# Order of the work beside the matmuls in the projections of a two-layer encoder step

## The chip, the cores and the metric

The kernel runs on one core of one Trainium2 chip. The metric is the device time of one execution in microseconds (us); less is better. The profile comes from one execution, recorded by the hardware profiler. Its names for the engines: PE is the TensorE's matmul side, PEld its loading of weights, DVE the VectorE, ACT the ScalarE, POOL the GpSimd, SP the SyncE, whose instructions issue DMAs. A suffix q (SPq, POOLq) means an engine's queue. Engines run side by side and wait for each other with semaphores; each works through its own instructions in order.

## The reference

A streaming encoder step of two layers, on a prompt of 2048 frames and 64 new frames of a running stream, with d = 1024, 16 heads of 64. Layer A: RMSNorm, one projection to q, k, v and gate, softmax attention over a band of 9 chunks of 64 frames with a learned bias on the relative distance, gate, output projection, residual. Then one projection to shared keys and values, and layer B: projection to q and gate, strictly causal stick-breaking attention over 2048 cached rows and the new ones, gate, output projection, residual, a last norm.

```python
def a_project(x, g, w_in):
    h = rms_norm(x, g)
    q, k, v, gate = jnp.split(h @ w_in, 4, axis=-1)
    return split_heads(q), split_heads(k), split_heads(v), gate

def shared_kv(x, g, w_kv):
    h = rms_norm(x, g)
    k, v = jnp.split(h @ w_kv, 2, axis=-1)

def sb_block(q, k, v, q_pos, k_pos):
    z = jnp.einsum('bqhd,bkhd->bhqk', q, k).astype(jnp.float32) * SCALE
    mask = (k_pos[None, :] < q_pos[:, None])[None, None]
    log_fail = jnp.where(mask, jax.nn.log_sigmoid(-z), 0.0)
    later = jnp.flip(jnp.cumsum(jnp.flip(log_fail, -1), axis=-1), -1) - log_fail
    w = jnp.where(mask, jnp.exp(jax.nn.log_sigmoid(z) + later), 0.0)
    return jnp.einsum('bhqk,bkhd->bqhd', w.astype(v.dtype), v)
```

The outputs are the two streams after the last norm, and the new keys and values of both layers, for the prompt and for the new frames. All is 32-bit.

## The kernel before

**Stages.** One after the other: the projections of A (about 0 to 760 us of the profiled span), band attention with A's output projection (to about 1497), the projections to the shared keys and values and B's q and gate (to about 2169), stick-breaking attention with the rest (to the end). The change is in the two runs of `projections`.

**Precision.** Every operand of a matmul is kept as two parts, high and low (`h`, `l`), whose sum is the 32-bit value; a `split` is a copy to the high part on ScalarE and a subtraction on VectorE for the low part. A product takes three matmuls for a block of 128 rows of weights: high by high, high by low, low by high.

**The pieces of `projections`.** The prompt is cut into two halves of 1024 frames. For each half:
- *values* (`values`): tiles of 128 frames by 512 columns, 24 matmuls each (`ps_v`). Half 0 has 18 (with the new frames), half 1 has 16. In the meantime the frames are normed (`normed`, GpSimd scales `xt`), transposed (`ps_tr`) and split (`parted`). The weights of values come in blocks (`block_rows`: DMA to `vraw`; `two_blocks`: scaled with the norm's gain to `vwh`, `vwl`). After each value `leave` splits and stores it; in B it stores the raw value (`v_raw<-vn`), and a tick later loads the rows shifted by one (`vps<-v_raw`), subtracts (`less`), splits (`vs`) and stores (`v_b<-vs`), since B's attention works on differences of values that stand next to each other.
- *mixing* (`mix`, beside the values): sums and differences of quarters of the frames, for the next item. Steps `one`, `two`, `three` for each of four pieces.
- *pairs* (`pair`): the columns of two heads for k, q or gate, in the manner of Strassen: P1 to P7, seven products of 12 matmuls instead of eight. Sums `c`, `u2` are made on VectorE. Two of the seven products reuse a PSUM bank, `ps_x` (P1, P3, P5, P7) and `ps_z` (P2, P4), once its content has been copied out (ScalarE, `c<-ps_x`, `c<-ps_z`) or added (VectorE). Half 0 of A has 12 pairs and half 1 has 8, B 12 and 4. In half 0 a pair also holds the 64 new frames (`new_frames`, `ps_q`, after P3). The heads are left as a split (`hl`) and stored by `put`.

**The weights of a pair** go through steps that are named in `weights_of`: `load` (two DMAs to `wraw`), `s1`, `s2` (four scalings each on GpSimd), `b1`, `b2` (splits of the upper and lower half: `ohh`, `ohl`; `olh`, `oll`), `-t1` to `-t4` (differences on GpSimd, written back to `wraw`) and `t1` to `t4` (splits of those; the profile shows `t1` as `x_new` in half 1 and the others as `t`). They are run between the products of earlier pairs: `this` is the pair of the products, `following` the next, `third` the one after; the raw tiles of `third` are those of `this`.

**Staged work.** Between the products, `all_pairs` starts jobs for later stages as room comes: `stage_cache` (loads a block of cached keys to `kr`, a few products later transposes it on TensorE into `ps_c`, splits to `ks`, stores; in A also the values `vr`), `stage_diff` (differences of cached values: `vvp`, `vvr`), `stage_w_out`, `stage_bias` (`bt`, stored to `bias`). A `tick` after each product lets the steps that wait in `waiting` move on.

**What sets the order.** The kernel is scheduled by Tile. A job's first step is its DMA, a later one its arithmetic. Inside `projections`, while `order.on` is set, every instruction on TensorE, VectorE, ScalarE and GpSimd is kept in the order in which the program makes it, and so are the DMAs made with `sp`, which is `order.engine(nc.sync)`. DMAs made with `nc.sync` itself go to the same engine, SyncE, where the scheduler chooses their place among the others. SyncE is one queue: a DMA whose data isn't ready holds what stands behind it.

```python
            def after(n, *steps):

                waiting.append([n, *steps])
                return waiting[-1]

            def tick():
                for x in waiting:
                    x[0] -= 1
                    if x[0] < 0:
                        x.pop(1)()
                        x[0] = 0
```

Of the kernel before, what the change touches and what calls it, by code (L numbers as in the profile page):

```python
# [16 lines left out]
P = 128  # L17
# [107 lines left out]
def encoder_step(ctx: ExitStack, tc: tile.TileContext, a: dict, o: dict):  # L125
# [143 lines left out]
    def projections(L, x_of, begin, w_v, cv, gv, out_v, jobs, first, prompt, sample, stages):  # L269
        with ExitStack() as own, ExitStack() as beside, ExitStack() as early:  # L270
# [61 lines left out]
            def fetched(t, pool, bufs):  # L332
                n = TOK[t][1]
                xt = pool.tile([P, D], F32, name="xt", tag="xt", bufs=bufs)
                sp.dma_start(xt[:n], x_of(t))
                return xt
# [31 lines left out]
            def block_rows(half, j, tag):  # L368
# [3 lines left out]
                sp.dma_start(raw, src.rearrange("(k p) c -> p k c", p=P))  # L372
# [16 lines left out]
            waiting, flight, seqs = [], [], [[*range(NK), len(TOK) - 1], [*range(NK, 2 * NK)]]  # L389
            seq, seq1 = seqs  # L390

            def after(n, *steps):

                waiting.append([n, *steps])
                return waiting[-1]

            def tick():
                for x in waiting:
                    x[0] -= 1
                    if x[0] < 0:  # L400
                        x.pop(1)()
                        x[0] = 0
                waiting[:] = [x for x in waiting if len(x) > 1]

            def values(hf, half, i, t, vws, pool, vps):
# [23 lines left out]
                def leave():  # L429
# [5 lines left out]
                    if L == "a":  # L435
                        store(out, sp.dma_start)
# [7 lines left out]
                    if L == "b":  # L444
                        sp.dma_start(vraw[1 + r0 : 1 + r0 + n, cols], vn)
                    sp.dma_start(dst[:, cols], vn)
                    if L == "a" or half and t in seqs[hf][-2:]:
                        return

                    prev = vps[i % 2]  # L450

                    def load():
                        if t == 0:
                            gps.memset(prev[0:1], 0.0)
                            for x, m in ((0, 112), (112, 15)):
                                sp.dma_start(prev[x + 1 : x + 1 + m], vraw[1 + x : 1 + x + m, cols])
                        elif n == NS:
                            sp.dma_start(prev[0:1], a["cache_b_v"][PAST - 1 : PAST, cols])
                            sp.dma_start(prev[1:n], vraw[1 + r0 : r0 + n, cols])
                        else:  # L460
                            sp.dma_start(prev, vraw[r0 : r0 + P, cols])

                    def less():
                        dve.tensor_tensor(prev[:n], prev[:n], vn, ALU.subtract)
                        store(prev[:n], sp.dma_start)

                    after(1, load, less)
# [3 lines left out]
            def weights_of(kind, w, c0, g, hp, raw, forms):  # L471
# [5 lines left out]
                def load():  # L477
                    for i, r in enumerate(raw):
                        sp.dma_start(r, w[i * CH : i * CH + CH, c : c + 2 * P].rearrange("(k p) c -> p k c", p=P))
# [6 lines left out]
                def whole(i):  # L486
                    split(*forms[i], raw[i].rearrange("p k (b c) -> p b k c", b=2))
                    if (kind, hp) in lay[L]["w"]:
                        for j, part in enumerate(forms[i]):
                            sp.dma_start(f32(lay[L]["w"][kind, hp][j, i]), f32(part))  # L490
# [32 lines left out]
            def pair(hf, kind, c0, hp, forms, pool, this, following, third, event):  # L523
# [14 lines left out]
                def leave(b, t0, src):  # L538
                    at = slice(r0 + t0 * CH, r0 + t0 * CH + CH)
                    hl = pool.tile([P, 2, CH], F32R, name="hl", tag="hl", bufs=HL[L, hf])  # L540
                    if kind == "g":
                        act.activation(f32(hl[:, 0]), src, AF.Silu)
                        sp.dma_start(lay[L]["g"][hp + b][:, at], f32(hl[:, 0]))
# [1527 lines left out]
```

## Time and profile before

| | before |
|---|---|
| median of 3 runs | 3414.68 us |
| lowest, highest run | 3414.37, 3416.91 us |
| the profiled execution | 3414.56 us |
| its span, first to last instruction | 3412.8 us |
| mean granted TensorE clock | 0.974 of full |
| DMA | 684.22 MB, 200 GB/s over the span |

A row of the profile names the line, the engine, the operation, what is written and what is read, and how many. Since nearly every instruction is made in one helper that keeps the order, nearly all rows stand at its line (L114); they are told apart by the names of the tiles. In the view of waits a row `PE ps_x <- ACT c` means that TensorE stood ahead of an instruction on `ps_x` until ScalarE had done one on `c`. In a timeline the number in brackets is the idle time just before the instruction, and after it what ended it.

### The profile page before, as it was taken

To read this page: it belongs to the slowest core of one execution; us is meant where nothing else is said; L and a number is where in the kernel's file an instruction comes from. 1 tells how busy PE (TensorE), PEld (TensorE's weight loads), DVE (VectorE), ACT (ScalarE), POOL (GpSimd) and SP (SyncE) were. 2 spreads that over 40 slices of the span, in tenths; PEclk is the share of its full clock that TensorE was granted. 3 is DMA by queue.
4 is the path that set the end of the run, shared out by engine and by line. 5 is a ranking of instruction groups with operands and counts; after the bars stand their busy time and mean duration, and the time that the engine had idled before them with its cause. 6 is when DMAs were issued, how large, how long until landed. Compare 5 with 4: busy or idle time off the path is not lost. (4 is left out here: it accounts for less than half of the span.)

```text
span 3412.8 us, 52013 instructions
## 1 busy us (share of the span) xinstructions
PE 3178.7 (93%) x16760; PEld 2644.0 (77%) x16760; DVE 2211.5 (65%) x3940; ACT 1870.0 (55%) x3743; POOL 1696.5 (50%) x2381
## 2 busy tenths in 40 slices
PE   7988998799998999997799987999999999999999
PEld 5766786578888888876678776788888887888877
DVE  4555445447777777236454555488887888888883
ACT  3333453337888777223354434366665667666663
POOL 3434535545565545014343325244466777777761
PEclk9989999999999999998899998999999999999999
DMA  4577654669799996446688765877755547455423
GB/s 159 171 254 253 216 182 178 224 213 254 219 255 278 240 234 184 149 158 226 215 304 299 258 237 187 266 218 196 211 171 158 154 110 221 135 159 149 127 76 117
DMA packets 476398, 684.22 MB, mean 200 GB/s; under 512 B 61105, under 2 KB 258257, under 8 KB 476126
## 3 DMA queue, kind: packets, MB, share of 16 engines
q1 hardware_dynamic: 473822, 672.51, 63.9%
q10 hardware_dynamic: 2304, 8.39, 0.7%
q8 instruction: 133, 2.18, 0.3%
q14 instruction: 139, 1.14, 0.1%
HBM read 422.01 MB, written 258.76 MB: 199 GB/s over the span
## 5 line engine op out<-in xcount | busy, mean ns | idle before, releaser
L114 DVE TENSOR_TENSOR pl<-wt,ph 128x512 fp32r<-128x512 f32 (+1 forms) x864 | 551.3, 653 | 108.0 <-ACT ph L114 104.0
L114 ACT ACTIVATE ph<-wt 128x512 fp32r<-128x512 f32 (+1 forms) x864 | 485.1, 578 | 189.8 <-PE wt L114 177.4
L114 PE MATMUL wt<-ident,s 128*128 128x128 f32 x3472 | 551.9, 274 | 9.4 <-DVE pl L114 7.2
L114 PEld LDWEIGHTS wt<-ident,s 128*128 128x128 f32 x3472 | 417.9, 141 | 84.0 <-DVE pl L114 13.1
L114 ACT ACTIVATE f<-z 128x512 f32<-128x512 f32 (+4 forms) x680 | 355.1, 536 | 191.4 <-PE z L114 124.7
L114 POOL TENSOR_TENSOR s<-f,s 128x256 f32<-128x256 f32 x416 | 361.3, 869 | 102.9 <-DVE s L114 94.8
L114 PE MATMUL acc<-ph,vt 128*128 128x512 f32 (+3 forms) x1088 | 374.3, 379 | 6.2 <-ACT ot L114 2.4
L114 PE MATMUL z<-kt,q 128*128 128x512 f32 (+3 forms) x1280 | 372.5, 378 | 3.3 <-ACT f L114 3.0
L114 PE MATMUL acc<-pl,vt 128*128 128x512 f32 (+3 forms) x1088 | 363.3, 367 | 9.3 <-DVE pl L114 9.0
L114 POOL TENSOR_TENSOR two<-f 128x256 f32<-128x256 f32 x416 | 260.1, 627 | 156.0 <-ACT f L114 140.8
L114 DVE TENSOR_TENSOR_SCAN s<-two,s,own 128x256 f32<-128x256 f32 x408 | 299.9, 737 | 34.0 <-POOL two L114 32.6
L114 POOL TENSOR_SCALAR s<-s,rc 128x640 f32<-128x640 f32 (+5 forms) x264 | 201.5, 768 | 235.2 <-DVE rc L114 140.3
L114 POOL TENSOR_TENSOR wraw<-wraw 128x512 f32<-128x512 f32 x96 | 141.3, 1482 | 276.4 <-DVE oll L114 199.4
L114 PEld LDWEIGHTS z<-kt,q 128*128 128x128 f32 x1280 | 220.1, 190 | 33.4 <-ACT f L114 9.9
L114 PE MATMUL ps_x<-x_own,t 128*128 128x512 f32 x864 | 225.6, 411 | 14.1 <-ACT c L114 13.7
L114 DVE CUSTOM_DVE_ANT_0 s<-z,bias 128x640 f32<-128x640 f32 (+4 forms) x256 | 184.7, 733 | 67.8 <-PE wt L114 52.2
L114 PEld LDWEIGHTS acc<-pl,vt 128*128 128x128 f32 x1088 | 193.9, 190 | 42.8 <-DVE pl L114 27.2
L114 DVE TENSOR_TENSOR_SCAN s<-f,own 128x128 f32<-128x128 f32 (+4 forms) x264 | 202.3, 787 | 30.1 <-ACT f L114 29.5
L114 PEld LDWEIGHTS acc<-ph,vt 128*128 128x128 f32 x1088 | 196.6, 190 | 29.0 <-ACT ph L114 8.4
L114 PE MATMUL ps_o<-big,oh 128*128 128x512 f32 x544 | 213.8, 393 | 0.0
L114 PE MATMUL ps_o<-bigl,oh 128*128 128x512 f32 x544 | 213.1, 392 | 0.0
L114 ACT ACTIVATE s<-s,mn 128x640 f32<-128x640 f32 (+5 forms) x264 | 200.4, 761 | 23.0 <-DVE mn L114 22.0
(248 smaller groups left out, 7159.4 us busy)
## 6 DMA issues: line engine op xcount, KB each, us to landing
vt<-v_b SPq DMA_DIRECT2D x80, 512.0 KB, 4.7
v_b<-vs SPq DMA_DIRECT2D x64, 512.0 KB, 3.1
q<-q_a SPq DMA_DIRECT2D x128, 256.0 KB, 5.4
q<-q_b SPq DMA_DIRECT2D x128, 256.0 KB, 4.3
vt<-v_a SPq DMA_DIRECT2D x48, 512.0 KB, 8.0
kt<-k_b SPq DMA_DIRECT2D x96, 256.0 KB, 5.8
v_a<-vs SPq DMA_DIRECT2D x40, 512.0 KB, 4.0
keys<-k_a SPq DMA_DIRECT2D x80, 256.0 KB, 6.9
```

Of the source, the lines that this page charges most:

```text
L114: ins = op(*args, **kwargs)
```

## The change

The edit changes no arithmetic of a matmul: TensorE has as many instructions as before, ScalarE too. VectorE has 2 fewer and GpSimd 2 more (two subtractions of values change engine), SyncE 2 more.

- All DMAs of `projections` and of the staged jobs are made with `nc.sync` instead of `sp`.
- In `pair`, a head's split and store go to a list, `lagging`, and run one product later, behind that product's sum. The weights' differences run about a product ahead of the splits that use them, and `s2` is set apart from `s1`.
- `after` takes a delay for each step. The subtraction on B's values runs two ticks after the load's tick instead of one; the slot of `vps` alternates on across the two column halves.
- The last three values of half 1 in B (before: two) aren't subtracted on the spot but staged (`new_diffs`).
- A mixing step runs with each value instead of two with some; the weight steps of the first pair are spread over more values.
- `bt` gets a second buffer (and `rel` shares it), `nn` loses one. At the start the loads are made where they are used.

```diff
-            def after(n, *steps):
+            def after(*steps):
-                waiting.append([n, *steps])
+                waiting.append([*steps])
                 return waiting[-1]
             def tick():
                 for x in waiting:
                     x[0] -= 1
                     if x[0] < 0:
                         x.pop(1)()
-                        x[0] = 0
+                        x.pop(0)
...
-                        sp.dma_start(vraw[1 + r0 : 1 + r0 + n, cols], vn)
-                    sp.dma_start(dst[:, cols], vn)
-                    if L == "a" or half and t in seqs[hf][-2:]:
+                        nc.sync.dma_start(vraw[1 + r0 : 1 + r0 + n, cols], vn)
+                    nc.sync.dma_start(dst[:, cols], vn)
+                    if L == "a" or half and t in seqs[hf][-3:]:
                         return
-                    prev = vps[i % 2]
+                    prev = vps[(half * len(seqs[hf]) + i) % 2]
...
-                    after(1, load, less)
+                    after(1, load, 1, less)
...
                 def leave(b, t0, src):
...
+                    def two():
+                        at = slice(r0 + t0 * CH, r0 + t0 * CH + CH)
+                        hl = pool.tile([P, 2, CH], F32R, name="hl", tag="hl", bufs=HL[L, hf])
+                        if kind == "g":
+                            act.activation(f32(hl[:, 0]), src, AF.Silu)
+                            nc.sync.dma_start(lay[L]["g"][hp + b][:, at], f32(hl[:, 0]))
+                            return
+                        split(hl[:, 0], hl[:, 1], src)
+                        put(L, kind, hp + b, at, hl)
...
+                    lagging.append(two)
...
                 times(x, quarter(hf, 0, 0), w11, True)
                 c1 = plain(x)
-                run(this, "t3", "t4")
+                run(this, "t2", "-t3")
+                lagged()
                 slot(0)
                 z = psum.tile([P, CH], F32, name="ps_z", tag="mm", bufs=5)
                 times(z, mixed(hf, 0), t1, True)
                 c5 = plain(z)
-                run(third, "load")
+                run(this, "t4")
+                run(following, "s2")
                 slot(1)
                 times(x, mixed(hf, 1), t2, False)
                 u2 = plain(x)
+                run(this, "t3")
                 slot(2)
+                run(third, "load")
                 if hf == 0:
                     nn = new_frames()
-                run(following, "b1", "-t1")
+                run(following, "b1")
                 slot(3)
                 times(z, mixed(hf, 2), w22, False)
                 dve.tensor_tensor(u2, z, u2, ALU.add)
-                rest = leave(1, 0, u2)
-                run(following, "t1")
-                rest()
                 if hf == 0:
                     new_turned(nn)
+                run(following, "-t1")
+                leave(1, 0, u2)
                 slot(4)
                 times(x, mixed(hf, 3), t3, False)
                 dve.tensor_tensor(c5, x, c5, ALU.add)
-                leave(1, 1, c5)()
+                run(following, "t1")
+                lagged()
+                leave(1, 1, c5)
                 slot(5)
                 y = psum.tile([P, CH], F32, name="ps_y", tag="mm", bufs=5)
                 times(y, quarter(hf, 1, 0), w21, True)
                 dve.tensor_tensor(c1, y, c1, ALU.add)
-                rest = leave(0, 0, c1)
-                run(following, "b2", "-t2")
-                rest()
+                run(following, "b2")
+                lagged()
+                leave(0, 0, c1)
+                run(third, "s1")
                 slot(6)
                 times(x, quarter(hf, 1, 1), t4, False)
-                last = plain(x) if kind == "k" and hf * HALF + CH - first >= 0 else x
-                rest = leave(0, 1, last)
-                run(following, "t2", "-t4", "-t3")
-                rest()
-                run(third, "s1", "s2")
+                if kind == "k" and hf * HALF + CH - first >= 0:
+                    x = plain(x)
+                run(following, "-t2", "-t4")
+                lagged()
+                leave(0, 1, x)
                 slot(7)
+                if not following:
+                    lagged()
...
-                    for _ in range((1, 1, 2, 2, 2, 2, 2, 0)[i]):
-                        mixing.pop(0)()
-                    if i == 3:
+                    for _ in range(1 + i % 2):
+                        if mixing:
+                            mixing.pop(0)()
+                    if i == 0:
                         raws = [raw_tiles()]
...
                         run(made[0], "load")
-                    if i == 5:
+                    if i == 2:
                         run(made[0], "s1")
+                    if i == 4:
+                        run(made[0], "b1", "s2")
                     if i == 6:
-                        run(made[0], "b1", "s2", "-t1")
+                        run(made[0], "-t1")
                     if i == 7:
                         run(made[0], "t1")
```

What the scheduler makes of it can be seen in the order of each engine. On SyncE, in A's pairs of half 0, before, where `kr` is the load of cached keys, `ks` their split on its way out, and `hl` a head:

```order
L114 DMA k_a_89<-ks 128x2x512
L114 DMA k_a_89<-hl 128x2x512
L114 DMA kr<-in_cache_a_k 128x4x128
L114 DMA vr<-in_cache_a_v 128x4x128
L114 DMA v_a<-vs 128x4x256
L114 DMA k_a_89<-hl 128x2x512
```

There the first job's `ks` is stored ahead of the second job's load. The same place after the change, where the `kr` is that of the third job:

```order
L911 DMA kr<-in_cache_a_k 128x4x128
L266 DMA k_a_90<-hl 128x2x512
L266 DMA k_a_89<-ks 128x2x512
L266 DMA k_a_90<-hl 128x2x512
L931 DMA v_a<-vs 128x4x256
L914 DMA vr<-in_cache_a_v 128x4x128
```

The load of a block of keys moved up by one job: it stands ahead of the store of the first job's `ks` instead of behind it and a head.

On VectorE, one pair of A's half 1 before, from the sum of P4 (`c<-ps_z`) past those of P5 (`c<-ps_x`) and P6 (`c<-ps_y`):

```order
L114 TENSOR_TENSOR c<-ps_z,c 128x512
L114 TENSOR_TENSOR x_new<-wraw,x_new 128x512
L114 TENSOR_TENSOR hl<-c,hl 128x512
L114 TENSOR_TENSOR vs<-vvp,vs 128x8x64
L114 TENSOR_TENSOR c<-ps_x,c 128x512
L114 TENSOR_TENSOR hl<-c,hl 128x512
L114 TENSOR_TENSOR c<-ps_y,c 128x512
L114 TENSOR_TENSOR oll<-wraw,olh 128x1024
```

And after:

```order
L114 TENSOR_TENSOR c<-ps_z,c 128x512
L114 TENSOR_TENSOR vs<-vvp,vs 128x8x64
L114 TENSOR_TENSOR c<-ps_x,c 128x512
L114 TENSOR_TENSOR x_new<-wraw,x_new 128x512
L114 TENSOR_TENSOR hl<-c,hl 128x512
L114 TENSOR_TENSOR c<-ps_y,c 128x512
L114 TENSOR_TENSOR oll<-wraw,olh 128x1024
L114 TENSOR_TENSOR hl<-c,hl 128x512
```

The cut of `t1` (`x_new`) and the head's rest (`hl`) moved behind the sum of P5.

On GpSimd, in the same pairs before; `x8` scalings are `s1` and `s2`, the others on `wraw` differences, `vvp` staged work:

```order
L114 TENSOR_TENSOR wraw<-wraw 128x4x128 x3
L114 TENSOR_SCALAR wraw<-wraw,g_a 128x256 x8
L114 TENSOR_TENSOR vvp<-vvp,vvr 128x512 x2
L114 TENSOR_TENSOR wraw<-wraw 128x4x128
L114 TENSOR_TENSOR vvp<-vvp,vvr 128x512
```

And after:

```order
L114 TENSOR_SCALAR wraw<-wraw,g_a 128x256 x4
L114 TENSOR_TENSOR vvp<-vvp,vvr 128x512
L114 TENSOR_TENSOR wraw<-wraw 128x4x128 x3
L114 TENSOR_SCALAR wraw<-wraw,g_a 128x256 x4
L114 TENSOR_TENSOR vvp<-vvp,vvr 128x512
L114 TENSOR_TENSOR wraw<-wraw 128x4x128
```

The eight scalings in a row became two lots of four, one ahead of the differences and one behind.

More of the change, by code (lines that the diff above doesn't have):

```diff
@@ L435, in leave @@
                     if L == "a":
-                        store(out, sp.dma_start)
+                        store(out, nc.sync.dma_start)
                     dst = out_v(t)
@@ L489, in whole @@
                         for j, part in enumerate(forms[i]):
-                            sp.dma_start(f32(lay[L]["w"][kind, hp][j, i]), f32(part))
+                            nc.sync.dma_start(f32(lay[L]["w"][kind, hp][j, i]), f32(part))
                 differ = dict(
@@ L552, in rest @@
                             dst = prompt[row : row + CH, (hp + b) * P : (hp + b) * P + P]
-                            after(1, partial(natural, pool, src, 0, P, 4, dst))
-                    return rest
+                            after(0, partial(natural, pool, src, 0, P, 4, dst))
+                    lagging.append(two)
                 def new_frames():
@@ L654, in event @@
                             begin()
-                            flight.append((after(3, *steps), tags))
+                            flight.append((after(3, steps[0], *(x for y in steps[1:] for x in (0, y))), tags))
                     following, third = ([*made[i + 1 :], {}, {}])[:2]
@@ L687, in values_beside @@
                 begin()
-                after(1, *steps)
+                after(1, steps[0], *(x for y in steps[1:] for x in (0, y)))
             todo = [
@@ L738, in projections @@
                         values_beside(i, ("ol", "xr"))
-                    if i in (4, 6):
-                        mixing = mix(0, (i - 4) // 2, [tmp[0], tmp[4 + (i - 4) // 2], tmp[1], tmp[2]])
-                    if 4 <= i < 8:
-                        for x in mixing[:2] if i % 2 == 0 else mixing[2:]:
-                            x()
                     if i == 6:
@@ L751, in projections @@
                     values(0, 1, i, t, vws, pool, vps)()
[L752 to L757 removed]
+                    if mixing:
+                        mixing.pop(0)()
                     if i == 1:
@@ L785, in projections @@
             made += [weights_of(*x, raws[i % 2], forms) for i, x in enumerate(todo[0]) if i]
-            run(made[1], "load", "s1", "s2")
+            run(made[1], "load", "s1")
             spaces = tc.tile_pool(name=f"s0_{L}", bufs=2, side="right")
@@ L887, in projections @@
             staging["pool"] = beside.enter_context(tc.tile_pool(name=f"s1_{L}", bufs=2))
-            run(made[0], "b2", "-t2", "t2", "-t4", "-t3")
-            run(made[1], "load", "s1", "s2")
+            run(made[0], "b2", "-t2", "-t4")
+            run(made[1], "load", "s1")
             all_pairs(1, todo[1], made, forms, spool, staging, {})
+            assert not staged[1]
             while waiting:
@@ L984, in cut @@
             split(vs[:, 0], vs[:, 1], raw)
-            sp.dma_start(f32(wod[k][:, :, cols]), f32(vs))
+            nc.sync.dma_start(f32(wod[k][:, :, cols]), f32(vs))
         return [load, cut]
@@ L1581, in encoder_step @@
     diffs = [("cache", t, i) for t in range(PAST // P) for i in range(2)]
-    new_diffs = [("new", t, 1) for t in (7, 16, 14, 15)]
+    new_diffs = [("new", t, 1) for t in (6, 7, 16, 13, 14, 15)]
     outs = [(k, half) for k in range(NK) for half in range(2)]
@@ L1782, in encoder_step @@
         o["b_k_s"],
[L1783 removed]
+        (beside_b, [staged_b, new_diffs[3:]]),
     )
```

129 lines of the change are left out of this document (58 added, 71 removed).

## The prediction

> **What bounds the kernel now.** I read the shares first, then the stages. The page's line of the TensorE, for the whole span:
>
> ```profile
> PE 3178.7 (93%) x16760; PEld 2644.0 (77%) x16760; DVE 2211.5 (65%) x3940; ACT 1870.0 (55%) x3743; POOL 1696.5 (50%) x2381
> ```
>
> TensorE works 93% of 3412.8 us and the other engines half to two thirds, so what can be gained is TensorE's idle time and its slow matmuls. The change touches the two `projections` stages, so I cut those into pieces with the view of busy time by windows: values of half 0, pairs of half 0, values of half 1, pairs of half 1, for mixer A and then B; the tenth row is one undisturbed pair of A.
>
> ```profile
> 22.30:139.90 117.60, 109.87 (x474) 87.20 (x473) 69.37 (x90) 44.97 (x81) 51.40 (x47) 0.96 0.41 142
> 139.90:455.30 315.40, 281.16 (x1297) 226.29 (x1296) 163.96 (x275) 130.55 (x231) 130.15 (x142) 0.96 0.68 227
> 458.60:564.60 106.00, 95.03 (x433) 76.85 (x431) 51.70 (x83) 42.94 (x76) 45.06 (x47) 0.97 0.51 184
> 564.60:759.80 195.20, 167.56 (x677) 129.84 (x677) 94.24 (x117) 79.45 (x132) 106.67 (x109) 0.96 0.63 215
> 1506.00:1634.90 128.90, 110.65 (x475) 88.67 (x474) 71.85 (x99) 51.09 (x92) 44.53 (x42) 0.89 0.62 213
> 1634.90:1949.10 314.20, 287.10 (x1394) 234.26 (x1393) 156.41 (x211) 145.27 (x250) 128.36 (x141) 0.96 0.78 272
> 1949.10:2071.20 122.10, 98.15 (x434) 78.88 (x432) 63.48 (x95) 45.91 (x81) 44.69 (x44) 0.90 0.65 226
> 2071.20:2168.80 97.60, 90.76 (x401) 72.63 (x401) 48.52 (x57) 44.58 (x74) 41.47 (x43) 0.94 0.60 203
> 413.50:435.20 21.70, 21.70 (x104) 17.74 (x103) 9.25 (x12) 9.95 (x17) 10.17 (x12) 1.00 0.44 153
> ```
>
> The columns are the window's length, busy us of PE, PEld, DVE, ACT and POOL, the granted clock, the DMA share and GB/s. The last row is what a pair of half 0 costs when nothing is waited for: 21.70 us, TensorE busy throughout at clock 1.00. A pair of half 1 has no new frames: seven products. The TensorE's timeline in half 1 of A shows the price of a product, with and without a wait ahead of it:
>
> ```profile
> 635.46 0.50 PE L114 MATMUL ps_x<-big,t 128*128 128x512 f32 x1 [2.89 <-DVE c L114]
> ...
> 639.90 0.40 PE L114 MATMUL ps_x<-big,ohh 128*128 128x512 f32 x1
> ...
> 642.66 2.92 PE L114 MATMUL ps_z<-x_own,x_new 128*128 128x512 f32 x12
> ...
> 652.72 0.73 PE L114 MATMUL ps_z<-x_own,olh 128*128 128x512 f32 x2 [4.35 <-ACT c L114]
> ...
> 657.16 2.96 PE L114 MATMUL ps_x<-x_own,t 128*128 128x512 f32 x12
> ```
>
> P1, from 639.90 to 642.66, takes 2.76 us for twelve matmuls. P7 ahead of it, after a wait of 2.89 us, took 4.44 us (635.46 to 639.90), and so did P4 after 4.35 us (652.72 to 657.16). So a wait of about 3 us or more costs itself **and 1.68 us** of slow matmuls. [...]
>
> With 2.76 us a product a pair of half 1 needs 19.4 us, and with 24 matmuls, 5.5 us, a value. From these, plus the small transposes seen in undisturbed stretches, I estimate what the eight windows would take with no wait: 105.6 (18 values), 267 (12 pairs, 18 cache flips at 0.38), 95 (16 values), 156 (8 pairs), 107, 271, 94.7 and 83.4 us. **Lost** today, window less estimate: 12, 48, 11, 39, 22, 43, 27 and 14 us, **216 us** in all. The view of TensorE's waits says on what, first for the stage of A (0 to 780 us), then of B (1480 to 2180):
>
> ```profile
> PE ps_c L114 <- DMA kr<-in_cache_a_k: 16.6, 5, 5.2
> PE ps_z L114 <- ACT c L114: 12.3, 6, 5.5
> PE ps_c L114 <- DMA kr<-in_cache_b_k: 11.5, 5, 5.6
> PE ps_x L114 <- ACT ohh L114: 10.5, 1, 10.5
> PE ps_x L114 <- ACT c L114: 9.6, 7, 2.2
> PE ps_x L114 <- DVE c L114: 8.8, 6, 2.9
> ```
>
> ```profile
> PE ps_v L114 <- ACT vwh L114: 20.8, 2, 11.0
> PE ps_x L114 <- ACT c L114: 19.7, 2, 14.0
> PE ps_x L114 <- ACT ohh L114: 14.2, 1, 14.2
> PE ps_c L114 <- DMA kr<-in_cache_b_k: 13.0, 7, 4.6
> PE ps_tr L114 <- POOL xt L114: 12.6, 2, 7.2
> ```
>
> Each row: us in total, times, longest. With the smaller rows and without the start they come to some 160 us; the other 56 are slow matmuls. All are waits on data that another engine gets to late; none of those engines is full.
>
> **The change, part by part.**
>
> *Cache keys (free SyncE order).* Ten flips in A waited 16.6 + 11.5 = 28.1 us for `kr`, seven in B 13.0. A `kr` load lands after
>
> ```profile
> DMA to landing us min/median/max: 2.9/5.0/8.2
> ```
>
> and is issued now behind stores that SyncE holds for their data, just ahead of its use. After, it stands a whole staged job earlier, right where the buffer comes free. Eighteen jobs in twelve pairs of 22 us are 14.7 us apart, more than 8.2, so the wait goes. With 1.68 us of slow matmuls each: 28.1 + 10 x 1.68 = 45 us in A's pairs of half 0 (of 48 lost there), 13.0 + 7 x 1.68 = 25 in B's.
>
> *Values of B (`less` a tick later).* The loop runs through SyncE, as its timeline shows:
>
> ```profile
> 1611.44 0.43 SPq L114 DMA_DIRECT2D vps<-v_raw  x1
> ...
> 1618.28 0.37 SPq L114 DMA_DIRECT2D vps<-v_raw  x1
> ```
>
> 6.84 us a round: the load goes out right behind the store `v_b<-vs` of the value before, which waits for that value's split, and lands in
>
> ```profile
> vps<-v_raw SPq DMA_DIRECT2D x27, 256.0 KB, 4.1
> ```
>
> then come the subtraction and the split. TensorE needs 5.5 us a value, so ScalarE falls 1.3 us behind with each, and at a stage's end TensorE stands for it: the waits on `vwh` (11.0 and 9.8), on `c` (14.0 at the first pair) and part of that on `ohh` (14.2). After, a whole value (5.5 us against the 4.1) lies between a load and its subtraction, the store ahead of the load is that of one value earlier, and ScalarE has no reason to stand there. The stage's weights then come at their own time. I count 20 of the 22 us lost in B's values of half 0, 16.7 of the 43 in the pairs behind it (14.0 and the 2.7 that its product ran slow), and, with the mixing spread out, 31 of the 41 (27 + 14) in half 1.
>
> *Pairs (order of ScalarE, VectorE, GpSimd).* The two waits quoted above. Ahead of 652.72:
>
> ```profile
> 641.01 4.68 POOL L114 TENSOR_TENSOR wraw<-wraw 128x512 f32<-128x512 f32 x3 [7.35 <-DVE oll L114]
> 645.67 4.63 POOL L114 TENSOR_SCALAR wraw<-wraw,g_a 128x256 f32<-128x256 f32 x8
> 650.25 2.49 POOL L114 TENSOR_TENSOR vvp<-vvp,vvr 128x512 f32<-128x512 f32 x2
> ...
> 651.55 0.63 ACT L114 ACTIVATE vs<-vvp 128x512 fp32r<-128x512 f32 x1 [4.67 <-POOL vvp L114]
> 652.09 0.58 ACT L114 ACTIVATE c<-ps_z 128x512 f32<-128x512 f32 x1
> ```
>
> GpSimd did three differences and eight scalings, 9.31 us in a row; `vvp` stood behind them, ScalarE's `vs` behind `vvp`, and the copy `c` that frees `ps_z` behind `vs`. After, four of the scalings come ahead of the differences, a product earlier (2.76 us), in GpSimd's 7.35 us of waiting: 4.68 + 2.32 = 7.0 us stand ahead of `vvp`, 2.3 less, and the differences follow a cut (`b2`) with less on VectorE ahead of it. 2.3 + 2.76 is more than the 4.35 waited, if that cut does come a product earlier; if not, 2 us stay. Ahead of 635.46:
>
> ```profile
> 633.13 1.07 DVE L114 TENSOR_TENSOR x_new<-wraw,x_new 128x512 fp32r<-128x512 f32 x1 [1.54 <-ACT x_new L114]
> ...
> 634.73 0.68 DVE L114 TENSOR_TENSOR c<-ps_x,c 128x512 f32<-128x512 f32 x1
> ```
>
> The sum `c`, which frees `ps_x`, stood behind `x_new` (the cut of `t1`) and a head's rest. After, sum first, then the rest: `x_new` waited 1.54 and took 1.07, so the sum comes at least 2.6 us earlier and the 2.89 goes. No instruction is added; each piece lies beside products of 2.76 us. With the mixing spread out and the first pair's weights moved ahead of the 10.5 us on `ohh` (and 1.7 of slow clock behind it), I count 37 of the 50 us (11 + 39) in A's half 1. What stays: the last mixing steps still stand ahead of the second product, some 4 us, and 1 us a pair.
>
> *A's values of half 0 and the start.* 10 of 12 us, for the same reasons as in B (less sure: here the loads are from the cache). At the start ScalarE stands for the gains:
>
> ```profile
> 13.53 1.33 ACT L114 ACTIVATE vwh<-vraw,g_a 128x512 fp32r<-128x512 f32 x2 [8.24 <-DMA g_a<-in_norm_a]
> ```
>
> `g_a` is now issued second instead of behind six loads, about 3 us earlier; the end of the chain moves as far: 3 us, at least 0, at most the 8.2 waited.
>
> *Bounds of what isn't seen.* Attention stages: a few instructions swap places there; no row prices that, so -5 to +5 us, and I take 0. DMA load: B's pairs of half 0 have share 0.78 of 314 us, 245 us; at 281 us that is 0.87, so landings may lengthen. Two subtractions go from VectorE to GpSimd, beside 50% idle: 0. The second `bt` buffer lets a store wait without holding VectorE: 0. Third weights: the load goes out after P3 and GpSimd wants it behind P6, so its landing,
>
> ```profile
> DMA to landing us min/median/max: 3.2/5.1/7.5
> ```
>
> meets 3 x 2.76 = 8.3 us less 1.5 for the cut: 6.8 us in half 1, 8.7 with the new frames. A longer one first uses up some 3 us until the cut of `t2` is due.
>
> **Sum** against the profiled execution (3414.56 us; the median of the runs is 3414.68): 3 + 10 + 36 + 37 + 20 + 33 + 31 = 170 us, where 36 and 33 are the pairs of half 0 with 1 us a pair left in. For waits in 36 pairs that I can't see I take off 0.6 us a pair, 22 us (between 0 and today's 4.0 in A's half 0, nearer to 0 because the causes are named). 3414.6 - 148 = **3266 us**.
>
> **Rivals.**
> - *Only the loads gain.* Staged steps stay in line ahead of the copies, and ScalarE waits for `vvp` or the late scalings as before. The keys (45 + 25) go, with a little of the values: gain 80, 3335 us. For it: the order has `vs<-vvp` still ahead of `c<-ps_z`. Against: the 9.31 us run on GpSimd is cut, and the sums come first on VectorE.
> - *The order is free but nothing comes earlier.* If loads still stand behind blocked stores, the keys' 70 us stay, and the rest comes: 3414.6 - 100 = 3315 us. Against: the order's rows.
> - *Slower: the third weights.* SyncE stays one queue, and a store that waits holds what follows:
>
> ```profile
> SPq L114 <- DVE vs L114: 228.1, 53, 14.9
> ```
>
>   53 such waits in A, longest 14.9 us. If the load of the third weights stands behind one of about 12 us in each pair, it is there 12 + 5.1 = 17 us after P3, 7 us past the 6.8 + 3. In 28 pairs that have a third, 28 x 7 = 196 us against 170 gained: about 3440 us. It decides from 10 us and turns the sign at 16. Against: mean wait 228.1 / 53 = 4.3 us.
>
> **Chances.** Forecast (gain 110 to 209) 0.62; only the loads 0.22; nothing earlier 0.07; no difference, as gains and new waits cancel, 0.04; slower 0.05. The low end takes all 216 + 3 us less 9, 3205; the high end takes in the loads' rival and reaches 20 us past it, 3355. A measurement tells 0.2%, 7 us, from no change: faster 0.91, same 0.04, slower 0.05.
>
> **What would show it.** In the changed profile the flips' waits on `kr` should be under 5 us in each stage; B's value loads 5.5 to 5.7 us apart; the waits on `vwh` and `ohh` in B under 5 us; pairs of A's half 1 at 20 to 21 us; the windows' clock at 0.98 or more. I am wrong if TensorE shows new rows of 2 us or more on `t`, or GpSimd waits for `wraw` loads in most pairs.

## The result and the profile after

| | before | after |
|---|---|---|
| median of 3 runs | 3414.68 us | 3262.03 us |
| the profiled execution, its span | 3414.56, 3412.8 us | 3262.03, 3260.2 us |
| mean granted clock | 0.974 | 0.989 |

The ratio is 0.9549 (95% interval 0.9528 to 0.9571): 152.6 us less, where 148 were forecast. TensorE's line of the page after:

```profile
PE 3142.9 (96%) x16760; PEld 2625.2 (81%) x16760; DVE 2229.5 (68%) x3938; ACT 1861.9 (57%) x3743; POOL 1717.8 (53%) x2383
```

As many matmuls, 35.8 us less busy (3178.7 to 3142.9) at a mean granted clock of 0.989 instead of 0.974, so fewer ran slowly; the other 117 us were idle. The view of busy time by windows follows, cut at the same places in the program (values, pairs, values, pairs of A, then of B). Its columns are the window's length, the busy us of PE, PEld, DVE, ACT and POOL with their instructions, the granted clock, the DMA share and GB/s:

```profile
16.00:123.40 107.40, 106.05 (x474) 85.14 (x473) 65.22 (x89) 44.38 (x80) 48.63 (x46) 1.00 0.45 161
123.40:399.80 276.40, 272.26 (x1314) 221.43 (x1313) 178.82 (x281) 130.87 (x236) 132.63 (x143) 1.00 0.81 269
399.80:495.70 95.90, 95.08 (x434) 76.99 (x433) 48.68 (x76) 39.77 (x71) 46.02 (x47) 1.00 0.49 181
495.70:663.20 167.50, 158.97 (x677) 127.52 (x676) 103.36 (x124) 80.83 (x136) 120.49 (x109) 0.98 0.73 249
1412.80:1524.60 111.80, 107.20 (x474) 86.16 (x473) 76.13 (x97) 50.47 (x91) 49.37 (x42) 0.97 0.72 239
1524.60:1814.90 290.30, 281.57 (x1394) 230.87 (x1393) 157.14 (x212) 143.22 (x253) 125.29 (x142) 0.99 0.87 300
1814.90:1913.40 98.50, 96.45 (x434) 78.41 (x433) 56.77 (x83) 41.41 (x74) 42.15 (x40) 0.98 0.72 247
1913.40:2015.70 102.30, 89.61 (x401) 71.71 (x400) 55.21 (x67) 47.11 (x81) 49.26 (x48) 0.92 0.64 215
```

Seven stages are shorter, four of A run at a clock of 0.98 or more, and the pairs of B's half 1 got longer: 102.3 us at a clock of 0.92 against 97.6 at 0.94. The largest rows of TensorE's waits, for A (0 to 720 us) and then B (1380 to 2100):

```profile
PE ps_tr L114 <- DVE xt L114: 7.0, 1, 7.0
PE ps_tr L114 <- POOL xt L114: 6.2, 3, 5.4
PE ps_z L114 <- ACT x_new L114: 5.9, 1, 5.9
```

```profile
PE ps_z L114 <- ACT x_new L114: 10.8, 1, 10.8
PE ps_x L114 <- ACT bigl L114: 8.7, 1, 8.7
PE ps_tr L114 <- POOL xt L114: 7.4, 2, 5.4
PE ps_v L114 <- ACT vwh L114: 4.3, 1, 4.3
```

No row on `kr` or `ohh` is left, and on `c` only one of 2.2 us in A. Two rows stand out instead, `x_new` and `bigl`, both at the first pair of a half. The 8.7 us on `bigl` stand at the same product as the 14.0 us on `c` before: of that wait 5.3 us went.

For comparison with the experiments, here is the time of each stage in the profiled executions of the two kernels and of the runs 1 to 9, from the start of its first product or value to that of the next stage's in TensorE's timeline; "first" is what precedes the first value, "A attention" begins with the first score:

| us | first | A values 0 | A pairs 0 | A values 1 | A pairs 1 | A attention | B values 0 | B pairs 0 | B values 1 | B pairs 1 |
|---|---|---|---|---|---|---|---|---|---|---|
| before | 22.3 | 117.7 | 318.7 | 106.0 | 203.8 | 737.6 | 128.9 | 314.2 | 122.1 | 98.1 |
| after | 16.0 | 107.4 | 276.4 | 95.9 | 176.2 | 741.0 | 111.8 | 290.3 | 98.5 | 104.8 |
| before, keys' loads free | 22.4 | 117.8 | 305.3 | 105.6 | 204.1 | 741.3 | 128.7 | 298.1 | 121.8 | 97.7 |
| before, all free | 21.9 | 118.4 | 307.2 | 106.8 | 203.6 | 738.8 | 124.4 | 289.3 | 109.9 | 96.5 |
| before, new pair | 22.2 | 118.3 | 297.8 | 105.6 | 170.8 | 736.3 | 127.6 | 306.3 | 121.2 | 98.6 |
| before, both | 22.0 | 118.3 | 290.2 | 106.0 | 172.9 | 738.9 | 123.2 | 287.7 | 110.3 | 97.5 |
| after, pinned | 16.5 | 106.6 | 292.3 | 95.4 | 174.3 | 739.6 | 112.1 | 296.9 | 94.6 | 103.9 |
| after, old pair | 16.9 | 106.4 | 286.3 | 96.0 | 208.0 | 739.0 | 111.8 | 296.0 | 94.7 | 106.3 |
| after, early subtraction | 15.9 | 106.0 | 279.7 | 96.0 | 179.4 | 739.7 | 111.6 | 288.8 | 96.8 | 101.4 |
| after, old mixing | 16.1 | 118.2 | 278.8 | 95.3 | 184.5 | 741.2 | 124.3 | 287.7 | 96.4 | 109.5 |
| after, one bt | 16.1 | 106.9 | 291.7 | 96.5 | 177.9 | 739.2 | 112.0 | 290.5 | 95.5 | 104.9 |

A stage that a run leaves alone moves by up to 3 to 4 us from one profile to the next; smaller differences are not read.

### The profile page after: what moved, and what is told of

Read it like the earlier page. It is cut to its first block, busy times and chain, and to the rows that moved or that the text cites. A ratio compares the mean times of both kernels' runs of the same rounds, so it can differ in the third digit from the quotient of the medians.

```text
span 3260.2 us, 52067 instructions
## 1 busy us (share of the span) xinstructions
PE 3142.9 (96%) x16760; PEld 2625.2 (81%) x16760; DVE 2229.5 (68%) x3938; ACT 1861.9 (57%) x3743; POOL 1717.8 (53%) x2383
## 4 chain that ended last, share of the span: by engine, by line
PE 39%; DVE 6%; issue 3%; DMA 2%; ACT 1%; POOL 1%; SPq 0%; ACTq 0%; POOLq 0%; DVEq 0%
PE acc L114 7%; PE z L114 6%; PE wt L114 6%; PE ps_j L114 5%; PE ps_x L114 5%; PE ps_o L114 3%; PE ps_z L114 3%; DVE s L114 2%; DVE pl L114 2%; PE ps_v L114 1%; PE ps_y L114 1%; PE ps_q L114 1%; DMA kt<-k_b 0%; ACT ph L114 0%; PE ps_n L114 0%
## 5 line engine op out<-in xcount | busy, mean ns | idle before, releaser
L114 POOL TENSOR_TENSOR s<-f,s 128x256 f32<-128x256 f32 x416 | 361.3, 869 | 104.0 <-DVE s L114 95.5
L114 DVE CUSTOM_DVE_ANT_0 s<-z,bias 128x640 f32<-128x640 f32 (+4 forms) x256 | 184.5, 732 | 70.6 <-PE wt L114 53.7
L114 POOL TENSOR_TENSOR rstd<-ms,nhalf 128x1 f32<-128x1 f32 (+1 forms) x51 | 33.8, 662 | 347.1 <-DVE ms L114 340.3
```

Source lines behind the costliest of these rows:

```text
L114: ins = op(*args, **kwargs)
```

## The experiments

**1. All DMAs free, in the kernel before.** Every DMA of `projections` and the staged jobs, as in the first line here. Median 3358.06 us, ratio 0.9829 (0.9812 to 0.9845).

```diff
-                sp.dma_start(xt[:n], x_of(t))
+                nc.sync.dma_start(xt[:n], x_of(t))
...
```

> The kernel before with every DMA of the projections and staged jobs made in SyncE's free order, all else old. If the cached keys' waits (28 + 13 us) hang on that order alone, as the forecast's sum has it, they go with the slow matmuls behind them, 70 us: 3330 to 3350 us, kr waits under 5 us in each stage. If it is the order of the other engines that counts (rival), 3400 to 3415 us, kr waits as before.

57 us, outside both ranges and less than the 70 of the keys alone in the sum, though the waits on `kr` are gone in both stages. In A's pairs of half 0 only 11.5 us came. VectorE's waits there (100 to 460 us) show one reason:

```profile
DVE bt L114 <- DMA bias<-bt: 27.6, 8, 8.7
```

Before, this row had 15.3 us in five waits. VectorE stands for the store of a bias tile (before the change such a store lands in a median of 2.4 us from its issue, in the kernel after, with free DMAs as here, in 5.0), and everything behind it in VectorE's order stands too: `nn`, and so TensorE's `ps_f` (13.1 us in four waits, against 2.3 in one). In B, where there is no bias, the pairs of half 0 gained 25 us. That is the number that the sum had for the keys, but run 2 shows that the keys alone bring 16 of it. The rest came with the wait on `c` at B's first pair, here in run 1 (1621 to 1911 us) and then in run 2 (1625 to 1924 us); before the change it was 14.0 us:

```profile
PE ps_x L114 <- ACT c L114: 5.2, 1, 5.2
```

```profile
PE ps_x L114 <- ACT c L114: 16.2, 1, 16.2
```

**2. Only the keys' loads free, in the kernel before.** In `stage_cache`, `kr` and `vr`. 3381.55 us, 0.9905 (0.9891 to 0.9920).

```diff
         def load():
-            sp.dma_start(kr, a[f"cache_{L}_k"][rows, cols].rearrange("(j p) c -> p j c", p=P))
+            nc.sync.dma_start(kr, a[f"cache_{L}_k"][rows, cols].rearrange("(j p) c -> p j c", p=P))
...
```

> The kernel before with only the two loads of stage_cache (kr, vr) in SyncE's free order. By the forecast's term: 45 us in A's pairs of half 0 and 25 in B's, about 3345 us, the same as with all DMAs free but for 10 us. Rival (the loads stay behind blocked stores, or the wait moves to another row): less than 20 us gained, over 3395 us.

33 us; both expectations missed. In B's pairs of half 0, 16.1 us came instead of 25. The 28.1 us on `kr` in A are gone, but the stage is only 13.4 us shorter. TensorE's waits in A's pairs of half 0 (140 to 446 us):

```profile
PE ps_f L114 <- DVE nn L114: 7.2, 4, 3.5
PE ps_x L114 <- ACT c L114: 6.4, 3, 4.3
PE ps_x L114 <- DVE c L114: 5.1, 3, 2.3
PE ps_x L114 <- DVE bigl L114: 2.5, 1, 2.5
PE ps_z L114 <- ACT c L114: 2.1, 1, 2.1
```

In the same stage before (139.9 to 458 us), below the two rows on `kr`:

```profile
PE ps_f L114 <- DVE nn L114: 2.3, 1, 2.3
PE ps_x L114 <- ACT c L114: 1.6, 1, 1.6
PE ps_z L114 <- ACT c L114: 1.2, 1, 1.2
PE ps_x L114 <- DVE bigl L114: 0.5, 1, 0.5
PE ps_x L114 <- DVE c L114: 0.4, 1, 0.4
```

23.3 us against 6.0. My reading: while TensorE stood for `kr`, VectorE and ScalarE caught up; without that pause TensorE stands for them.

The other part is the slow matmuls, which the sum put behind every flip (the transposes of a block of cached keys). TensorE's timeline before the change has flips with and without them:

```profile
186.92 1.09 PE L114 MATMUL ps_c<-ident,kr 128*128 128x128 f32 x4 [3.01 <-DMA kr<-in_cache_a_k]
187.66 5.36 PE L114 MATMUL ps_x<-x_own,t 128*128 128x512 f32 x12
...
258.23 0.63 PE L114 MATMUL ps_c<-ident,kr 128*128 128x128 f32 x4 [2.44 <-DMA kr<-in_cache_a_k]
258.62 3.03 PE L114 MATMUL ps_z<-big,bigl 128*128 128x512 f32 x12
```

Four of the ten flips that waited in A have slow matmuls behind them, and two of the seven in B. From the distances of the matmuls' starts I estimate some 10 and 4 us, where the sum has 10 x 1.68 = 17 and 7 x 1.68 = 12. With 13.0 + 4 us B's term comes to 17, by this estimate, close to the 16.1 measured.

**3. The new order inside a pair, in the kernel before.** 3353.72 us, 0.9831 (0.9814 to 0.9847). The body of `pair`, with `lagging`, is that of the change; DMAs stay pinned.

> The kernel before with only the new order inside a pair, DMAs pinned as before. Taken out of the new kernel this part costs 39 us; if the parts simply add, it gives 39 here: about 3375 us, kr waits in A as before (28 us). If the new order also lets the stores at the head of SyncE's queue go sooner, so that the pinned loads behind them come earlier (rival to the forecast's claim that the keys need the free order), 3345 to 3362 us with kr waits in A under 18 us. If other waits take the place of those removed, over 3390 us.

59 us, the second expectation: 33 in A's pairs of half 1, 21 in those of half 0, 8 in B's, nothing in B's half 1. The keys' waits in A fell with the loads still pinned:

```profile
PE ps_c L114 <- DMA kr<-in_cache_a_k: 10.1, 6, 3.8
PE ps_c L114 <- DMA kr<-in_cache_b_k: 5.8, 2, 5.0
```

15.9 us instead of 28.1. SyncE's queue waited less for heads in that stage, where the first row is the new pair (140 to 440 us) and the second the kernel before (140 to 460):

```profile
SPq L114 <- DVE hl L114: 46.6, 30, 4.4
```

```profile
SPq L114 <- DVE hl L114: 67.2, 27, 6.6
```

My reading: a head that is split a product later is also stored a product later in the program, so its data is nearer to ready when the store comes to the queue's head, and the loads behind it go sooner.

**4. Both of these, in the kernel before.** 3312.90 us, 0.9702 (0.9684 to 0.9719).

> The kernel before with both parts that were run alone: the new order inside a pair (alone -59 us) and every DMA of the projections and staged jobs in SyncE's free order (alone -57 us). If the two removed different waits, -116 us: about 3297 us. If both shortened the same waits of the pairs of half 0 (keys behind stores that wait for heads), as the 11 and 39 us say that they cost when taken out of the new kernel, they add to less: 3315 to 3335 us, A's pairs of half 0 at 285 to 297 us, no shorter than with either alone by more than some 10 us, since bt has one buffer here.

104 us, not 116: the two overlap by 12, most of it in the pairs of half 0: in A 20.9 and 11.5 us alone and 28.5 together, in B 7.9 and 24.9 alone and 26.5 together. A's stage came out inside what was expected, and is still 14 us longer than after the change; run 9 shows by what in the main.

**5. The DMAs pinned again, in the kernel after.** 3273.11 us, 0.9585 (0.9570 to 0.9599); the reverse of the diff of 1.

> The kernel after with these DMAs pinned in program order again, all else new. By the forecast's sum it loses the keys' 70 us and the start's 3 to 6: 3330 to 3345 us, with kr waits of some 40 us. Rival (the new order of the other engines alone brings the loads early enough): 3262 to 3280 us.

Only 11 us lost: the rival. TensorE's waits on `kr` come to 18.4 us instead of some 40. By stage, 16 and 7 us in the pairs of half 0, while B's values of half 1 got 4 shorter. So the free order, worth 57 us alone, is worth 11 on top of the rest.

**6. The old pair, in the kernel after.** 3300.98 us, 0.9666 (0.9651 to 0.9680). `leave`, the body of `pair` and the first pairs' steps as before.

> The kernel after with the old order inside a pair (heads right behind their sum, the weights' differences and splits where they were), all else new. By the forecast the pair's order is worth most of what the pairs of half 1 lost (A some 28 us, B some 8) and 10 us in the pairs of half 0: 3300 to 3320 us, A's half 1 at 24 us a pair. Rival (free loads do it for the pairs too): 3262 to 3275 us.

39 us, as forecast: 32 in A's pairs of half 1, 10 and 6 in those of half 0, with the waits on `c` back (33 us in A). B's half 1 lost 1.5, not 8.

**7. The subtraction a tick earlier, in the kernel after.** 3256.53 us, 0.9542 (0.9527 to 0.9557).

```diff
-                    after(1, load, 1, less)
+                    after(1, load, 0, less)
```

> The kernel after with the subtraction on B's values one tick behind its load's tick again, all else new. If the late subtraction is what lets ScalarE keep up in B, as the forecast's sum has it (20 in B's values of half 0, some 17 at the first pair behind them, part of the 31 in half 1), 3295 to 3315 us and B's values of half 0 at 124 us or more. Rival (the free order of the loads does it alone, and the late tick only makes the first pair wait for the last store): 3250 to 3265 us.

The rival: nothing is lost, and B's values of half 0 take 111.6 us, against 111.8 in the kernel after. On top of the rest, the late subtraction, on which the forecast put 20 us and more, brings nothing that can be measured, and the wait on `bigl` at the first pair is shorter without it (6.2 us against 8.7). Its worth alone isn't shown. TensorE's waits on `vwh` in B were 20.8 us before and 6.7 with the free order alone (1); with the DMAs pinned they are 21.1 in run 3, with the early subtraction and the old mixing, and 4.3 in run 5, with the late one and the new mixing. So free order is enough to shorten that wait, and the late subtraction may be a second way to it; a run without either, in the kernel after, wasn't made.

**8. The old pace of the mixing, in the kernel after.** In half 0's frames two steps at once with one value and one with the next, as before; in half 1 the old pace too, though there the new one also puts two steps with every second value. 3293.54 us, 0.9651 (0.9637 to 0.9666).

```diff
+                    if i in (4, 6):
+                        mixing = mix(0, (i - 4) // 2, [tmp[0], tmp[4 + (i - 4) // 2], tmp[1], tmp[2]])
+                    if 4 <= i < 8:
+                        for x in mixing[:2] if i % 2 == 0 else mixing[2:]:
+                            x()
...
-                    if i >= 4:
-                        mixing.pop(0)()
...
-                    for _ in range(1 + i % 2):
-                        if mixing:
-                            mixing.pop(0)()
+                    for _ in range((1, 1, 2, 2, 2, 2, 2, 0)[i]):
+                        mixing.pop(0)()
```

> The kernel after with the old pace of the mixing steps in both stages (two at once in half 0's values; in half 1 up to two a value, begun a value later), the weight steps as in the new one. By the forecast the pace is what removed the 10.5 and 14.2 us on the first product of half 1: 3285 to 3300 us with that wait back on ohh or x_new. Rival (the weights' earlier steps did it): 3255 to 3268 us.

By the ratios 0.0102 of the kernel before, some 35 us, as forecast in total: 10.8 in A's values of half 0, 12.5 in B's, 8 and 5 in the pairs of half 1. TensorE's wait on `x_new` rose from 5.9 to 11.7 us in A and from 10.8 to 15.5 in B, but no wait on `ohh` came back, and the values of half 1 stayed as short as after (95.3 and 96.4 us): the pace isn't what removed the waits on `ohh`. In half 0 it is the mixing that held the values, and this run's timelines of GpSimd, ScalarE and TensorE in B's values of half 0 show how:

```profile
1472.16 5.03 POOL L114 TENSOR_TENSOR bigl<-x_own,x_own 128x512 f32<-128x512 f32 x4
1483.78 0.54 POOL L114 TENSOR_TENSOR rstd<-ms,nhalf 64x1 f32<-64x1 f32 x1 [6.58 <-DVE ms L114]
1484.42 1.85 POOL L114 TENSOR_SCALAR xt<-xt,rstd 64x1024 f32<-64x1024 f32 x1
```

```profile
1477.78 0.63 ACT L114 ACTIVATE big<-bigl 128x512 fp32r<-128x512 f32 x1 [7.62 <-DVE bigl L114]
```

```profile
1486.32 1.11 PE L114 MATMUL ps_tr<-ident,xt 64*128 64x64 f32 x8 [5.78 <-POOL xt L114]
```

The first row is a mixing step. The second step of the same value puts its sums on VectorE and its splits on ScalarE, which stands 7.62 us for them; the norm of the new frames (`ms`) comes behind them, `xt` is late, and TensorE waits with its transposes. The kernel before has the same rows of GpSimd 74 us later.

**9. One buffer for `bt`, in the kernel after.** 3274.94 us, 0.9598 (0.9582 to 0.9614).

```diff
-            bt = pool.tile([P, 640], F32, name="bt", tag="bt", bufs=2)
+            bt = pool.tile([P, 640], F32, name="bt", tag="bt", bufs=1)
```

> The kernel after with one buffer for bt, as before (rel in a place of its own again). The forecast priced the second buffer at nothing: 3260 to 3265 us. Rival: with the stores in free order VectorE stands for the store of the bias ahead, as in the kernel before with free order (27.6 us there in A's pairs of half 0, and 13 us of TensorE behind nn): 3272 to 3285 us, lost in A's pairs of half 0 alone.

The rival again: 17 us by the ratios, 15.3 of them in A's pairs of half 0. VectorE's waits there (100 to 460 us):

```profile
DVE bt L114 <- DMA bias<-bt: 23.4, 6, 6.5
```

**10. The mixing of half 1 a value faster, in the kernel after.** 3259.32 us, 0.9549 (0.9531 to 0.9568).

```diff
-                    for _ in range(1 + i % 2):
-                        if mixing:
-                            mixing.pop(0)()
+                    if i == 7:
+                        run(made[0], "t1")
+                    for _ in range((2, 1, 2, 1, 2, 2, 1, 0)[i]):
+                        mixing.pop(0)()
```

> The kernel after with the mixing of half 1 a value faster, so that its last step is done a value before the pairs, and the split of t1 ahead of the values' last steps. If TensorE's waits on x_new (5.9 us in A, 10.8 in B) come from the last mixing steps standing ahead of that split on ScalarE and VectorE, most of them and the slow matmuls behind them go: 3243 to 3253 us. Rival (GpSimd or VectorE is full in those values, and the wait moves to them): 3258 to 3268 us.

No difference. The waits on `x_new` went from 5.9 to 4.5 us and from 10.8 to 8.5 only; in B the last splits of the mixing and the subtractions of the values, one behind the other on VectorE and ScalarE, still stand ahead of `x_new`.

**11 and 12. Four values staged, with 7; and these two with 10.** 3255.74 us, 0.9539 (0.9525 to 0.9553), and 3253.51 us, 0.9533 (0.9514 to 0.9551).

```diff
-                    if L == "a" or half and t in seqs[hf][-3:]:
+                    if L == "a" or half and t in seqs[hf][-4:]:
...
-    new_diffs = [("new", t, 1) for t in (6, 7, 16, 13, 14, 15)]
+    new_diffs = [("new", t, 1) for t in (5, 6, 7, 16, 12, 13, 14, 15)]
```

> The kernel after with the subtraction one tick behind its load again and the last four values of half 1 staged instead of three. If the first pair of B waits because its copy c stands for the store of the last values' differences (v_b), whose buffer it takes over, that store now goes out two values earlier, and the waits on bigl (8.7 us) and part of that on x_new (10.8) go: ratio 0.950 to 0.953. Rival (the staged jobs cost as much among the pairs, or the wait is for something else): 0.954 to 0.957.

> As the run with four staged values and the early subtraction, and in addition the mixing of half 1 a value faster with t1 split ahead of the last steps. If the waits on x_new come from the mixing and the values' differences together, both are gone now: ratio 0.948 to 0.951. Rival (nothing left in them): the same as without, within 0.001.

Both lie below the kernel after, but inside its interval: they are not told apart from it, nor from each other. What they aimed at is the wait on `bigl` in the kernel after, here in the order of time SyncE's last store of a difference, ScalarE's first copy of the pairs, and TensorE:

```profile
1532.72 0.48 SPq L427 DMA_DIRECT2D v_b<-vs  x1
```

```profile
1538.16 0.60 ACT L114 ACTIVATE c<-ps_x 128x512 f32<-128x512 f32 x1 [6.19 <-DMA v_b<-vs]
```

```profile
1539.33 4.58 PE L114 MATMUL ps_x<-big,bigl 128*128 128x512 f32 x12 [8.71 <-ACT bigl L114]
```

The pairs' pool is opened where the values' pool was closed, so `c` waits until the last tile in its place has been stored, and the split `bigl` waits in line behind `c`. With four staged ScalarE's copy waits for the store of the new frames' values instead, as it does already with the early subtraction alone (5.74 us in run 7):

```profile
1534.72 0.60 ACT L114 ACTIVATE c<-ps_x 128x512 f32<-128x512 f32 x1 [7.74 <-DMA out_b_v_s<-vn]
```

TensorE's wait on `bigl` fell from 8.7 us to 6.2 in run 7, 5.2 in run 11 and 4.7 in run 12, and that on `x_new` from 10.8 to 8.5 and 7.5 in the last two. That the places are the same memory was read from the pools and this wait; a run with places of their own wasn't made.

## Why the prediction was right, and where its steps were not

The time (3266 forecast, 3262 measured), the sign and the range were right. That the time came so near is in part luck, since errors of opposite sign cancel: by the table the start and the eight stages gained 154.5 us, where the terms add up to 170, and the discount of 22 us, put there for waits that can't be seen, takes off more than the difference.

| gain, us | start | A values 0 | A pairs 0 | A half 1 | B values 0 | B pairs 0 | B half 1 |
|---|---|---|---|---|---|---|---|
| forecast | 3 | 10 | 36 | 37 | 20 | 33 | 31 |
| measured | 6.3 | 10.3 | 42.3 | 37.7 | 17.1 | 23.9 | 16.9 |

- *What bounds the kernel*: right. 216 us were put down as lost to waits and slow matmuls of the projections; 148 of them went (the eight columns of values and pairs in the table of stages, 1409.5 less 1261.3), and the 3.4 us more in A's attention lay inside the bounds given. A wait's extra cost in slow matmuls held where the wait is long: P2 behind the 5.9 us on `x_new` took from 504.48 to 509.18, 4.70 us against 2.76. In that stretch the granted clock was 0.57. Before the change matmuls ran slow behind a wait of 3.01 us too (run 2; clock 0.50 from 188 to 192.5 us). TensorE's busy time fell by 35.8 us, where the prediction counted 56 us of slow matmuls in all.
- *Cache keys, 70 us by the free order*: the waits went, the step's price was wrong. In B it was 16 instead of 25 (2): 1.68 us of slow matmuls were put behind every flip, though the flips there waited 1.9 us on average and the price was read from waits of about 3 us or more. In A it was 13.4 instead of 45 (2), for that reason and because waits of TensorE on other engines, 17 us more than before, took the place of those on `kr`. The free order isn't the only way to them either: the pair's order shortens them too (3), which fits that taking the free order out again costs only 11 us (5). A's pairs of half 0 came out near their term (42.3 for 36) through `bt`, the pair's order and the free order together, not through the keys' 45; that is luck.
- *Pairs of B's half 0*: by the prediction's own 43 lost less 1 us for each of 12 pairs the term is 31, not 33. Of the 16.7 us counted for the wait on `c` at the first pair, most stayed: the product there now waits 8.7 us, on `bigl`.
- *Values of B, by the late subtraction*: the step that failed. The chain through SyncE was there, 6.84 us a round, and ScalarE was late; but the later subtraction isn't needed to remove the wait (7), and the loads didn't come a value apart (they start at 1452.22, 1463.05, 1471.10 and 1474.20 us). In half 0 what held TensorE was mostly the mixing, two steps at once ahead of the norm (8): 12.5 of the 17 us. The free order alone brought 4.5 there and 12.2 in half 1 (1). The 14.2 us on `ohh` mostly moved on to `x_new` (10.8) and its slow matmuls, so that values and pairs of half 1 together gained 16.9 instead of 31.
- *Pairs*: right. The run on GpSimd ahead of `vvp` was forecast at 4.68 + 2.32 us; in half 1 of A after the change it is

```profile
547.37 4.68 POOL L114 TENSOR_TENSOR wraw<-wraw 128x512 f32<-128x512 f32 x3
552.03 2.28 POOL L114 TENSOR_SCALAR wraw<-wraw,g_a 128x256 f32<-128x256 f32 x4
554.28 1.29 POOL L114 TENSOR_TENSOR vvp<-vvp,vvr 128x512 f32<-128x512 f32 x1
```

  A's half 1 gained 37.7 us (37 forecast), and an undisturbed pair takes 19.3 (P7's starts at 520.81 and 540.13). The products that take over a bank are P3, P5 and P7 on `ps_x` and P4 on `ps_z`, four and not two; the waits quoted stand at P7 and P4. In half 0 the pair's order was worth 21 us alone, where the sum had next to nothing for it.
- *A's values and the start*: 10.3 us (10 forecast), but by the mixing (8), not by the loads and the subtraction as in B: the number is luck. The first value starts 6.3 us earlier (3 forecast).
- *`bt`, priced at nothing*: 15 to 17 us in the kernel after (9). The row was there before the change, "DVE bt <- DMA bias", 15.3 us in five waits; it was given no price.
- *Rivals*: "only the loads gain" is refuted by 3 and 6, "nothing comes earlier" by 1 and 2, where the rows on `kr` go. The slower one did not come, though GpSimd does now wait for the third weights in A,

```profile
POOL wraw L114 <- DMA wraw<-in_w_in_a: 25.7, 9, 6.0
```

  2.9 us each on average, 6.0 at most, against the 3 us that were left until the cut is due. TensorE's rows on `t` stay under the 2 us that were named as a sign of being wrong (1.6 and 0.9 us in A, 1.4 in B).
- *The discount of 22 us for waits that can't be seen*: what is left are `x_new` (5.9 and 10.8) and `bigl` (8.7), 25.4 us before their slow matmuls, at the first pairs, not 0.6 a pair. Part of that is old waits, those on `ohh` and `c`, in a new place.
- *The signs that were named*: the waits on `kr` are gone, that on `vwh` in B is 4.3 us and that on `ohh` is gone, and A's pairs of half 1 take 20.9 us on average by the window of 167.50 us, as forecast. The value loads 5.5 to 5.7 us apart did not come, and the clock is under 0.98 in two windows of B (0.97 and 0.92).

What stays open: what shortened the values of half 1 (in B 98.5 us against 110.3 with both parts of 4, in A 95.9 against 106.0). The pace of the mixing is ruled out (8), and the first pair's earlier weights, which end the wait on `ohh`, are likely, but they and the third staged value were not tried alone. The late subtraction was only taken out, never put in alone.

## What to carry to other kernels

Waits of the engine that sets the end were not additive here: without the 28.1 us on `kr`, A's pairs of half 0 were 13.4 us shorter (2). So price a removed wait with what the other engines would be late with next, and look at their own waits, even those of an engine that is half idle, if it works in a pinned order and something on the path stands behind. Two parts that attack the same wait by different ways can each be worth much alone and less on top of the other (the free order 57 us alone and 11 on the rest, the pair's order 59 and 39), so a part's value needs both runs, in alone and out alone. Where a store holds a buffer, a second one can pay (17 us for `bt`, run 9), and the row "engine <- DMA of its own output" (23.4 us there) names the place.

## What the runs showed of the hardware

In B's pairs of half 0 more was moved at once after the change, and the cached keys landed sooner, not later. The DMA share rose from 0.78 to 0.87 and the rate from 272 to 300 GB/s, while their loads took a median of 4.2 us from issue to landing instead of 5.2, and at most 6.4 instead of 8.2. Not all transfers did: the stores of q's heads there took 5.9 us instead of 3.1. Why is not shown.

Whether matmuls run slow behind a short wait doesn't follow from its length alone. In the kernel before, the products behind a wait of 2.85 us (at 204.13 us) ran at a granted clock of 1.00 (204.52 to 209.40 us), while twelve matmuls behind one of 1.90 us (at 1885.18) took 4.42 us at 0.61, from 1885.57 to 1889.99, instead of 2.76.
